# Attention weights kept in four tiles and stored from the diagonal; the keys' low parts formed for two heads at once

## The chip, the cores and the metric

The kernel runs on one core of a Trainium2 chip. The time is the device time of one execution in microseconds (us). A profiled execution shows the instructions of each engine: TensorE (PE, with its weight loads as a row of their own, PEld), VectorE (DVE), ScalarE (ACT), GpSimd (POOL), and SyncE (SP), whose queue issues most of the transfers between HBM and the on-chip memory. A time in a row counts from the first instruction, and L12 is line 12 of the kernel's file.

## The reference, cut to what matters

One layer of a transformer-like block over 1024 tokens of width 1024, all in float32: a layer norm, one input projection, two groups of heads that read it (4 gated-delta heads of 128 and 8 forgetting-attention heads of 64), an output projection, and a large MLP. The change touches the forgetting attention alone:

```python
def block(args):
    i, q_i, c_i = args
    s = jnp.einsum('bqhd,bkhd->bhqk', q_i, k).astype(jnp.float32) * scale
    s = s + c_i[..., :, None] - c_all[..., None, :]
    q_pos = i * Q_BLOCK + jnp.arange(Q_BLOCK)
    s = jnp.where(k_pos[None, :] <= q_pos[:, None], s, -jnp.inf)
    attn = jax.nn.softmax(s, axis=-1)
    return jnp.einsum('bhqk,bkhd->bqhd', attn.astype(v.dtype), v)
```

`c_all` is the running sum of the forget gates' logarithms. The scores are causal, in blocks of 128 queries.

## The kernel before, in words

TensorE multiplies in a rounded form of float32 (`F32R`). To come near full float32, an operand x is split into a high part (x rounded, by a copy on ScalarE) and a low part (x minus the high part, by `split_lo`, a subtraction on VectorE, L54), and a product becomes two or three matmuls: high with high, high with low, low with high.

The stages follow one another: layer norm and values, the projections in columns (`proj_ch`, L211, matmuls at L218), the gated-delta heads, the forgetting attention, the output projection (`tok_mm`, L955, matmuls at L958), and the MLP. The framework orders the instructions of each engine by priorities when the kernel is built, and each engine then runs its own list in that order; a load waits in SP's queue until its buffer is free, and what stands behind it waits too. The z projections (`z_proj`, L452, `gz` in the rows) have a late priority and fill TensorE while attention waits.

The attention (L701 to L902) is a loop over 64 steps (`steps`, L871): 8 heads times 8 query blocks r, in the order 0, 1, 4, 5, 2, 3, 6, 7. The parts of a step are spread over the loop's turns: `fox_a` of a step, `fox_b` of the step before, `fox_c` and `fox_d` of those before them.

- `fox_start` (L841) calls `fox_load` for a head, and for an even head `fox_values` for both heads of the pair. It is called four steps ahead of the head. `fox_load` (L710) brings in the head's queries and keys from `qk_spill`, each twice, to partitions 0 to 63 and 64 to 127 (L715, two tiles `raw` of tag `qk_raw`, of which there are two buffers). `qa` holds the high part of the queries above their low part (L719, L720), `ka` the high part of the keys twice (L721), `kl` the low part of the keys twice (L722, the `kl` rows of L54), and `cb` the gate sums, read to all partitions (L724). The tiles of even heads lie in the pool `fh[0]`, those of odd heads in `fh[1]`. The values of a pair (`vr`, L729) use tag `qk_raw` too, as do the raw loads of `gdn_mix` (L854).
- `fox_a` makes the scores of a query block, in one or two chunks of at most 512 keys: 128 rows of `qa` with `ka` (L753: high and low queries with high keys), 128 rows of `qa` with `kl` (L754: high and low queries with low keys), and where the chunk holds the diagonal, the causal mask as a bf16 matmul with the identity (L756). VectorE adds `cb` and takes the minimum (L758); ScalarE takes the exponential (L761).
- `fox_b` transposes the weights of the block, 128 by 128 (L783), into PSUM; ScalarE casts them into `pth`, the high part (L785), and VectorE subtracts into `ptl`, the low part (L786, rows of L54). Two query blocks, r = 2g and r = 2g + 1, make a group g and share the tiles `pth` and `ptl`, of shape [128, kmax, 2, 128]: key block, query block of the group, query. Groups 0 and 1 use tiles with kmax 4, groups 2 and 3 tiles with kmax 8, one buffer each. Key block nk - 1 (nk = 2g + 2) lies above the diagonal for the group's first query block, and GpSimd writes zeros there for each group (L776, L777).
- `fox_c` multiplies the values of each key block with the weights of both query blocks, for `pth` and `ptl` (L797), and `fox_d` transposes the result back (L808).

```python
pth = pool.tile([P, kmax, 2, P], F32R, tag=f"pt_hi{kmax}", name=f"pth{h}_{g}", bufs=1)
ptl = pool.tile([P, kmax, 2, P], F32R, tag=f"pt_lo{kmax}", name=f"ptl{h}_{g}", bufs=1)
nc.gpsimd.tensor_copy(out=pth[:, nk - 1, 0], in_=zero)
nc.gpsimd.tensor_copy(out=ptl[:, nk - 1, 0], in_=zero)
```

Elsewhere in the kernel nearly every matmul takes 128 rows. The one exception is a transpose of 50 rows ahead of the column stage (L339, `crow`, between the transposes of L167 and the value projection of L320).

Of the kernel before, what the change touches and what calls it, by code (L numbers as in the profile page):

```python
# [8 lines left out]
F32 = mybir.dt.float32  # L9
F32R = mybir.dt.float32r  # L10
# [5 lines left out]
P = 128  # L16
T = 1024
# [15 lines left out]
def _sl(i, n=P):  # L33
    return slice(i * n, (i + 1) * n)
# [3 lines left out]
def tile_block(ctx: ExitStack, tc: tile.TileContext, x, p, ln_in_g, ln_in_b, w_in, conv_w, a_log, dt_bias,  # L38
               gdn_norm_g, b_f, fox_norm_g, w_out, ln1_g, ln1_b, w_up, w_down, w_ple, w_ple_gate,
               b_ple_gate, ln2_g, ln2_b, out):  # L40
    nc = tc.nc
    PS = bass.MemoryType.PSUM
    x, p, out = x[0], p[0, 0], out[0]
# [9 lines left out]
    def split_lo(eng, lo, src, hi):  # L53
        eng.tensor_tensor(out=lo, in0=src, in1=hi.bitcast(F32), op=ALU.subtract)  # L54
# [27 lines left out]
    ident = cpool.tile([P, P], F32, name="ident")  # L82
# [3 lines left out]
    zero = cpool.tile([P, P], F32, name="zero")  # L86
# [17 lines left out]
    qk_spill = tc.dram_tile([2, 4, P, T], F32, name="qk_spill")  # L104
# [72 lines left out]
    def pj(name):  # L177

        return psd.tile([P, 512], F32, tag="pj", name=name)

    def sm(name):
        return psx.tile([P, 512], F32, tag="sm", name=name)
# [40 lines left out]
    with tc.tile_pool(name="start", bufs=2, reuse_waits="tile") as stp:  # L223
# [10 lines left out]
        pt = stp.tile([P, NT, DPLE], F32, name="p_raw", bufs=1)  # L234
# [35 lines left out]
        pth = stp.tile([P, 2, T], F32R, name="pT_hi", bufs=1)  # L270
        ptl = stp.tile([P, 2, T], F32R, name="pT_lo", bufs=1)
# [35 lines left out]
        for t in range(NT):  # L307
            if t + 3 < NT:
                load_x(t + 3)
            h = stp.tile([P, D], F32, tag="h", name=f"h{t}")  # L310
# [5 lines left out]
            for n in range(2):  # L316
                ps = pj(f"psv{t}")
                for k in range(NK):
                    for wi, (a, w) in enumerate(((act_hi, wv_hi), (act_hi, wv_lo), (act_lo, wv_hi))):
                        nc.tensor.matmul(ps[:, 0:264], a[t // 4][:, t % 4, k], w[:, k, _sl(n, 264)],  # L320
                                         start=(k == 0 and wi == 0), stop=(k == NK - 1 and wi == 2))
# [16 lines left out]
        ps = sm("ps_cols")  # L338
# [121 lines left out]
    for i in range(1, 3):  # L460
        nc.sync.dma_start(out=img[i].rearrange("(q r i) -> q r i", q=32, i=P),
                          in_=zero[0:32].unsqueeze(1).to_broadcast([32, GH * HST // (32 * P), P]))
# [239 lines left out]
    fp = fst.enter_context(tc.tile_pool(name="fox", bufs=2, reuse_waits="tile"))  # L702
    fh = [fst.enter_context(tc.tile_pool(name=f"foxh{j}", bufs=1, reuse_waits="tile")) for j in range(2)]
    fvp = fst.enter_context(tc.tile_pool(name="foxv", bufs=2, reuse_waits="tile"))
    frs = ExitStack()
    fr = frs.enter_context(tc.tile_pool(name="foxr", bufs=2, side="right", reuse_waits="tile"))
# [3 lines left out]
    def fox_load(h):  # L710
        pr, j = h // 2, h % 2
        raw = [fp.tile([P, T], F32, tag="qk_raw", name=f"qkr{h}_{w}", bufs=2) for w in range(2)]
        for w in range(2):
            for half in range(2):
                nc.sync.dma_start(out=raw[w][_sl(half, 64)], in_=qk_spill[w, pr, _sl(j, 64), :])  # L715
        qa = fh[j].tile([P, T], F32R, tag="qa", name=f"qa{h}")
        ka = fh[j].tile([P, T], F32R, tag="ka", name=f"ka{h}")
        kl = fh[j].tile([P, T], F32R, tag="kl", name=f"kl{h}")
        nc.scalar.copy(out=qa, in_=raw[0])  # L719
        split_lo(nc.vector, qa[64:128], raw[0][64:128], qa[64:128])  # L720
        nc.scalar.copy(out=ka, in_=raw[1])  # L721
        split_lo(nc.vector, kl, raw[1], ka)  # L722
        cb = fh[j].tile([P, T], F32, tag="cb", name=f"cb{h}")
        nc.sync.dma_start(out=cb, in_=row_spill[32 + h * 8:40 + h * 8, :].rearrange("c i -> (c i)").partition_broadcast(P))  # L724
        return qa, ka, kl, cb
# [11 lines left out]

    heads, pairs, tiles = {}, {}, {}

    def fox_a(h, r):  # L740

        j = h % 2
        qa, ka, kl, cb = heads[h]
        W = (r + 1) * P
        s = tiles[h, r] = fr.tile([P, T], F32, tag="s", name="s", bufs=2)
        m = fr.tile([P, 2], F32, tag="m", name="m", bufs=4)

        cut = min(W, 512) if W != 640 else 384
        for i, (n0, n1) in enumerate([(0, max(cut, 256)), (cut, W)][:1 + (W > 512)]):
            e = min(W, n1)  # L750
            diag = n0 <= r * P < n1
            ps = psf.tile([P, 512], F32, tag="sc", name="ps_sc")
            nc.tensor.matmul(ps[:, :n1 - n0], qa[:, _sl(r)], ka[:, n0:n1], start=True, stop=False)  # L753
            nc.tensor.matmul(ps[:, :n1 - n0], qa[:, _sl(r)], kl[:, n0:n1], start=False, stop=not diag)  # L754
            if diag:
                nc.tensor.matmul(ps[:, r * P - n0:(r + 1) * P - n0], identb, mask_f, start=False, stop=True)  # L756

            nc.vector.tensor_tensor_reduce(out=s[:, n0:e], in0=ps[:, :e - n0], in1=cb[:, n0:e], scale=1.0,  # L758
                                           scalar=3.0e38 if i == 0 else m[:, 0:1],
                                           op0=ALU.add, op1=ALU.min, accum_out=m[:, i:i + 1])  # L760
        nc.scalar.activation(out=s[:, :W], in_=s[:, :W], func=AF.Exp, bias=m[:, i:i + 1], scale=-1.0,  # L761
                             accum_out=pairs[h // 2][2][:, r, j:j + 1])

    def fox_b(h, r):

        g, rr = r // 2, r % 2
        nk = 2 * g + 2
        s = tiles.pop((h, r))
        if rr == 0:
            kmax = 4 if g < 2 else 8  # L770
            pool = fvp if kmax == 4 else fr
            pth = pool.tile([P, kmax, 2, P], F32R, tag=f"pt_hi{kmax}", name=f"pth{h}_{g}", bufs=1)
            ptl = pool.tile([P, kmax, 2, P], F32R, tag=f"pt_lo{kmax}", name=f"ptl{h}_{g}", bufs=1)
            tiles[h, "p"] = pth, ptl

            nc.gpsimd.tensor_copy(out=pth[:, nk - 1, 0], in_=zero)  # L776
            nc.gpsimd.tensor_copy(out=ptl[:, nk - 1, 0], in_=zero)  # L777
        pth, ptl = tiles[h, "p"]
        for k0 in range(0, r + 1, 4):
            kn = min(4, r + 1 - k0)  # L780
            pt = psf.tile([P, 512], F32, tag="pt", name="ps_pt").rearrange("q (c i) -> q c i", i=P)
            for i in range(kn):
                nc.tensor.transpose(pt[:, i], s[:, _sl(k0 + i)], ident)  # L783
            hi = pth[:, k0:k0 + kn, rr]
            nc.scalar.copy(out=hi, in_=pt[:, :kn])  # L785
            split_lo(nc.vector, ptl[:, k0:k0 + kn, rr], pt[:, :kn], hi)  # L786

    def fox_c(h, g):

        j = h % 2  # L790
        nk = 2 * g + 2
        va = pairs[h // 2][0]
        pth, ptl = tiles.pop((h, "c", g))
        po = psf.tile([P, 512], F32, tag="av", name="ps_av", bufs=1)
        for kb in range(nk):
            for i, pt in enumerate((pth, ptl)):
                nc.tensor.matmul(po[:, 0:256], va[j][:, kb].rearrange("q a d -> q (a d)"),  # L797
                                 pt[:, kb].rearrange("q a b -> q (a b)"),
                                 start=(kb == 0 and i == 0), stop=(kb == nk - 1 and i == 1))
        ot = tiles[h, "o", g] = fr.tile([P, 256], F32, tag="ot", name="ot")  # L800
        nc.scalar.copy(out=ot, in_=po[:, 0:256])
# [39 lines left out]
    def fox_start(h):  # L841
        heads[h] = fox_load(h)
        if h % 2 == 0:
            va = fox_values(h // 2)
            if h < 6:
                osb = fr.tile([P, 8, 2, DH], F32, tag="osb", name=f"osb{h}", bufs=3)
            else:
                osb = fvp.tile([P, 8, 2, DH], F32, tag="va", name=f"osb{h}", bufs=3)
            pairs[h // 2] = (va, osb,
                             fr.tile([P, 8, 2], F32, tag="ls", name=f"ls{h}"))  # L850
# [24 lines left out]
    for i in range(n + 12):  # L875
        if i < n:
            h, r = steps[i]
# [5 lines left out]
        if 1 <= i <= n:  # L883
            h, r = steps[i - 1]
# [3 lines left out]
        if 2 <= i < n + 2:  # L888
            h, r = steps[i - 2]
            if r % 2:  # L890
                fox_c(h, r // 2)
        if 3 <= i < n + 3:
            h, r = steps[i - 3]
# [97 lines left out]
    for t in range(NT):  # L991
        h1 = hpool.tile([P, D], F32, tag="h1", name=f"h1_{t}")
        nc.sync.dma_start(out=h1, in_=h_spill[_sl(t), :])
        j = t % 4
# [3 lines left out]
        for n in range(2):  # L998
            ps = early.get((t, n))
            if ps is None:  # L1000
                ps = pj("ps_mix")
# [312 lines left out]
    b = [bank("ps_db") for bank in (pj, pj, pj, sm)]  # L1314
    a = [sm("ps_da") for _ in range(4)]
# [110 lines left out]
    for js in ((0, 1), (2,), (3,)):  # L1426
        w = P * len(js)
        m = 512 // w
        for c0 in range(0, NP, m):
            r = x0[:, count["r"] % 4]  # L1430
# [4 lines left out]
            for i in range(m):  # L1435
                for wi, (x, y) in enumerate(((0, 0), (0, 1), (1, 0))):
                    for j in js:
                        nc.tensor.matmul(b[j], rs[x][:, i, _sl(j - js[0])], Q[c0 + i][y],  # L1438
                                         start=(c0 == 0 and i == 0 and wi == 0),
                                         stop=(c0 + i == NP - 1 and wi == 2))  # L1440
# [39 lines left out]
```

## Time and profile before

| | us |
|---|---|
| median of 3 runs (1426.23 to 1431.31) | 1428.26 |
| the profiled execution | 1429.82 |
| its span, first to last instruction | 1427.9 |
| TensorE busy, matmuls | 1381.4 |
| TensorE busy, weight loads | 1167.2 |
| VectorE busy | 1106.8 |
| ScalarE busy | 560.7 |
| GpSimd busy | 29.6 |

Busy time is the union of an engine's instructions. Matmuls are pipelined, and the end of each is modelled, so that a busy TensorE need not be at its peak; the distance from one start to the next says more. A row of the timeline gives start, duration, engine, line, operation, the tiles written and read, the shapes and, in brackets, the idle time of the engine before it and what ended that. "issue" means that nothing in the profile ended it. A share is given for the span; the page that goes with the profile gives the granted TensorE clock as full nearly throughout.

### The profile page before, as it was taken

The numbers are of one execution on the slowest core, as the hardware profiler recorded it, in microseconds if no ns is written. First come the engines' busy times: TensorE is split into PE (matmuls) and PEld (weight loads), VectorE is DVE, ScalarE is ACT, GpSimd is POOL, SyncE is SP. The second block draws the span as 40 slices with busy tenths as digits, with TensorE's granted clock in tenths as the row PEclk, the third lists the DMA queues.
The fourth block names the chain that finished last, engine by engine and source line by source line (L and its number), as shares of the span: only waits on it lengthen the run. The fifth ranks groups of instructions, "written<-read, shape, count | busy, mean of one in ns | idle before, by whom it ended". The sixth has DMA issues, their size and how long they took to land.

```text
span 1427.9 us, 20552 instructions
## 1 busy us (share of the span) xinstructions
PE 1381.4 (97%) x7342; PEld 1167.2 (82%) x7342; DVE 1106.8 (78%) x2326; ACT 560.7 (39%) x1024; POOL 29.6 (2%) x84
## 2 busy tenths in 40 slices
PE   7999989999999999899999999999999999999997
PEld 5988868988887888778889888888888888888885
DVE  6858799689478989968998677776667799747877
ACT  4324412241247777631134233333334444555421
POOL 1000000000000111100000000000000000000000
PEclk9999999999999999999999999999999999999999
DMA  9866425444553433433567744444445994334342
GB/s 301 247 178 208 133 76 130 150 159 122 136 167 112 132 99 115 141 121 129 198 232 220 222 158 162 142 150 148 137 159 197 315 325 147 96 96 126 114 137 81
DMA packets 195868, 229.09 MB, mean 160 GB/s; under 512 B 23877, under 2 KB 128566, under 8 KB 195766
## 3 DMA queue, kind: packets, MB, share of 16 engines
q1 hardware_dynamic: 186374, 221.48, 49.1%
q10 hardware_dynamic: 9008, 5.24, 1.4%
q8 instruction: 58, 0.95, 0.3%
q0 software_dynamic: 384, 1.06, 0.2%
q14 instruction: 44, 0.36, 0.1%
HBM read 152.14 MB, written 75.60 MB: 159 GB/s over the span
## 4 chain that ended last, share of the span: by engine, by line
PE 47%; DMA 4%; DVE 4%; issue 1%; ACT 0%; SPq 0%; DVEq 0%; ACTq 0%
PE ps_uP L1212 21%; PE ps_da L1332 9%; PE ps_db L1332 9%; PE ps_db L1438 3%; PE ps_mix L958 2%; DMA hb<-h_spill 1%; PE ps_gP L1079 1%; DVE h L51 1%; DMA r<-t_spill 1%; PE ps_tr L965 1%; DMA h_spill<-h 1%; DMA h<-h_spill 1%; DVE gv L51 0%; DVE st L140 0%; DMA wo_raw<-in_w_out_dram 0%
## 5 line engine op out<-in xcount | busy, mean ns | idle before, releaser
L1212 PE MATMUL ps_uP<-T,uS 128*128 128x512 f32 x576 | 133.9, 390 | 1.3 <-ACT ua L1217 1.3
L1212 PEld LDWEIGHTS ps_uP<-T,uS 128*128 128x128 f32 x576 | 108.1, 188 | 24.9 <-ACT ua L1217 1.7
L1302 ACT CAST rh<-rr 128x512 fp32r<-128x512 f32 x112 | 69.8, 623 | 139.6 <-PE ps_db L1332 51.9
L54 DVE TENSOR_TENSOR rl<-rr,rh 128x512 fp32r<-128x512 f32 x112 | 76.8, 687 | 60.3 <-ACT rh L1302 25.6
L1212 PE MATMUL ps_uP<-B,uA 128*128 128x512 f32 x384 | 92.2, 395 | 0.0
L1212 PEld LDWEIGHTS ps_uP<-B,uA 128*128 128x128 f32 x384 | 72.1, 188 | 17.3
L958 PE MATMUL ps_mix<-wo,act_hi 128*128 128x512 f32 x256 | 81.9, 396 | 0.3 <-ACT act_hi L838 0.3
L218 PE MATMUL g<-act_hi,in_hi 128*128 128x512 f32 x192 | 76.1, 396 | 5.0 <-DVE edge L431 5.0
L218 PE MATMUL g<-act_hi,in_lo 128*128 128x512 f32 x192 | 75.7, 396 | 1.1 <-DVE in_lo L54 1.1
L218 PE MATMUL g<-act_lo,in_hi 128*128 128x512 f32 x192 | 75.8, 395 | 0.0
L1302 ACT CAST rl<-B 128x512 fp32r<-128x512 f32 x96 | 59.6, 622 | 24.6 <-PE ps_db L1332 12.1
L54 DVE TENSOR_TENSOR uA<-uraw,uA 128x512 fp32r<-128x512 f32 x48 | 33.0, 689 | 46.2 <-ACT uA L1207 46.2
L1207 ACT CAST uS<-wS 128x512 fp32r<-128x512 f32 x64 | 39.5, 622 | 73.1 <-issue 48.2
L54 DVE TENSOR_TENSOR ql<-B,rl 128x512 fp32r<-128x512 f32 x96 | 65.5, 684 | 0.3
L54 DVE TENSOR_TENSOR ptl<-ps_pt,pth 128x512 fp32r<-128x512 f32 (+2 forms) x96 | 51.0, 551 | 8.7 <-ACT pth L785 8.0
L958 PEld LDWEIGHTS ps_mix<-wo,act_hi 128*128 128x128 f32 x256 | 47.4, 188 | 10.2 <-DVE wo L54 0.6
L51 DVE SCALAR_TENSOR_TENSOR cv<-g,hcw,cv 128x510 f32<-128x510 f32 (+2 forms) x72 | 53.2, 739 | 1.5 <-ACT cv L424 1.1
L785 ACT CAST pth<-ps_pt 128x512 fp32r<-128x512 f32 (+2 forms) x96 | 43.5, 480 | 22.1 <-PE ps_pt L783 21.0
L1332 PE MATMUL ps_da<-ql,rh 128*128 128x512 f32 x192 | 51.3, 389 | 0.0
L1332 PE MATMUL ps_db<-rl 128*128 128x512 f32 x192 | 51.3, 389 | 0.0
L1332 PE MATMUL ps_da<-rl 128*128 128x512 f32 x192 | 51.3, 389 | 0.0
L761 ACT ACTIVATE s<-s,m 128x128 f32<-128x128 f32 (+3 forms) x64 | 50.0, 781 | 3.4 <-DVE m L758 3.2
(369 smaller groups left out, 3628.6 us busy)
## 6 DMA issues: line engine op xcount, KB each, us to landing
uraw<-in_w_up_dram SPq DMA_DIRECT2D x32, 512.0 KB, 4.4
B<-in_w_down_dram SPq DMA_DIRECT2D x32, 512.0 KB, 5.3
rr<-rS SPq DMA_DIRECT2D x64, 256.0 KB, 2.8
in_raw<-in_w_in_dram SPq DMA_DIRECT2D x24, 512.0 KB, 4.1
rr<-rA SPq DMA_DIRECT2D x48, 256.0 KB, 2.8
h_spill<-h SPq DMA_DIRECT2D x16, 512.0 KB, 3.9
qkr<-qk_spill SPq DMA_DIRECT2D x32, 256.0 KB, 4.1
rA<-ub SPq DMA_DIRECT2D x32, 256.0 KB, 2.1
```

What stands on the lines that cost most here:

```text
L51: nc.vector.scalar_tensor_tensor(out=o, in0=a, scalar=s, in1=b, op0=op0, op1=op1)
L54: eng.tensor_tensor(out=lo, in0=src, in1=hi.bitcast(F32), op=ALU.subtract)
L218: mm = nc.tensor.matmul(ps, w[:, k, :], a[n][:, :, k], start=(k == 0 and wi == 0), stop=(k == NK - 1 and wi == 2))
L761: nc.scalar.activation(out=s[:, :W], in_=s[:, :W], func=AF.Exp, bias=m[:, i:i + 1], scale=-1.0, accum_out=pairs[h // 2][2][:, r, j:j + 1])
L785: nc.scalar.copy(out=hi, in_=pt[:, :kn])
L958: nc.tensor.matmul(ps, a[t // 4][:, t % 4, k], w, start=(k == 0 and wi == 0), stop=(k == NK - 1 and wi == 2))
L965: nc.tensor.transpose(ps[:, k], row[:, _sl(k)], ident)
L1207: nc.scalar.copy(out=hi, in_=a[s])
L1212: nc.tensor.matmul(ps[p], w[:, k], B[t][b][k], start=(chain is None and k == 0 and wi == 0), stop=(k == 3 and wi == 2), skip_group_check=c ...
L1302: nc.scalar.copy(out=hi, in_=src)
L1332: nc.tensor.matmul(ps[j], rs[x][:, _sl(j)], qs[y], start=(not chain and c == 0 and wi == 0), stop=(c == NP - 1 and wi == 2), skip_group_ch ...
L1438: nc.tensor.matmul(b[j], rs[x][:, i, _sl(j - js[0])], Q[c0 + i][y], start=(c0 == 0 and i == 0 and wi == 0), stop=(c0 + i == NP - 1 and wi ...
```

## The change

Two edits, both in the attention.

The weights' tiles are made once, ahead of the loop: a high and a low tile of kmax 4 and of kmax 8. They are kept for all heads. The key blocks are stored in reverse, from the diagonal back: key block kb of a group lies at place nk - 1 - kb. The place above the diagonal of the group's first query block is then always place 0, and GpSimd zeroes it once in each of the four tiles, 4 copies where there were 64. The transposes of a chunk are issued in reverse order, and `fox_c` reads place nk - 1 - kb.

The low part of the keys is formed once for a pair of heads. `qk_spill[1, pr]` holds the keys of both heads, 64 partitions each; for an even head they are loaded as they lie into a further raw tile of tag `qk_raw` (one load of 128 partitions), copied by ScalarE and subtracted in place by VectorE. The odd head takes over the tile, which lies in `fh[pr % 2]`. The second score matmul takes only the 64 partitions of its own head: high queries with low keys. To have the high queries on the same partitions, the low part of the queries goes to partitions 64 to 127 for an even head and 0 to 63 for an odd one. The product of the two low parts is no longer computed.

```diff
         qa = fh[j].tile([P, T], F32R, tag="qa", name=f"qa{h}")
         ka = fh[j].tile([P, T], F32R, tag="ka", name=f"ka{h}")
-        kl = fh[j].tile([P, T], F32R, tag="kl", name=f"kl{h}")
         nc.scalar.copy(out=qa, in_=raw[0])
-        split_lo(nc.vector, qa[64:128], raw[0][64:128], qa[64:128])
+
+        lo = _sl(1 - j, 64)
+        split_lo(nc.vector, qa[lo], raw[0][lo], qa[lo])
         nc.scalar.copy(out=ka, in_=raw[1])
-        split_lo(nc.vector, kl, raw[1], ka)
+        if j == 0:
+
+            kr = fp.tile([P, T], F32, tag="qk_raw", name=f"qkr{h}_l", bufs=2)
+            nc.sync.dma_start(out=kr, in_=qk_spill[1, pr])
+            kl = fh[pr % 2].tile([P, T], F32R, tag="kl", name=f"kl{h}")
+            nc.scalar.copy(out=kl, in_=kr)
+            split_lo(nc.vector, kl, kr, kl)
+        else:
+            kl = heads[h - 1][2]
...
+    weights = []
+    for kmax, pool in ((4, fvp), (8, fr)):
+        weights.append([pool.tile([P, kmax, 2, P], F32R, tag=f"pt_{part}{kmax}", name=f"pt{part[0]}{kmax}", bufs=1)
+                        for part in ("hi", "lo")])
+        for w in weights[-1]:
+            nc.gpsimd.tensor_copy(out=w[:, 0, 0], in_=zero)
...
-            nc.tensor.matmul(ps[:, :n1 - n0], qa[:, _sl(r)], kl[:, n0:n1], start=False, stop=not diag)
+            nc.tensor.matmul(ps[:, :n1 - n0], qa[_sl(j, 64), _sl(r)], kl[_sl(j, 64), n0:n1], start=False, stop=not diag)
...
         if rr == 0:
-            kmax = 4 if g < 2 else 8
-            pool = fvp if kmax == 4 else fr
-            pth = pool.tile([P, kmax, 2, P], F32R, tag=f"pt_hi{kmax}", name=f"pth{h}_{g}", bufs=1)
-            ptl = pool.tile([P, kmax, 2, P], F32R, tag=f"pt_lo{kmax}", name=f"ptl{h}_{g}", bufs=1)
-            tiles[h, "p"] = pth, ptl
-
-            nc.gpsimd.tensor_copy(out=pth[:, nk - 1, 0], in_=zero)
-            nc.gpsimd.tensor_copy(out=ptl[:, nk - 1, 0], in_=zero)
+            tiles[h, "p"] = weights[g // 2]
         pth, ptl = tiles[h, "p"]
         for k0 in range(0, r + 1, 4):
             kn = min(4, r + 1 - k0)
             pt = psf.tile([P, 512], F32, tag="pt", name="ps_pt").rearrange("q (c i) -> q c i", i=P)
+            m0 = nk - k0 - kn
             for i in range(kn):
-                nc.tensor.transpose(pt[:, i], s[:, _sl(k0 + i)], ident)
-            hi = pth[:, k0:k0 + kn, rr]
+                nc.tensor.transpose(pt[:, i], s[:, _sl(k0 + kn - 1 - i)], ident)
+            hi = pth[:, m0:m0 + kn, rr]
             nc.scalar.copy(out=hi, in_=pt[:, :kn])
-            split_lo(nc.vector, ptl[:, k0:k0 + kn, rr], pt[:, :kn], hi)
+            split_lo(nc.vector, ptl[:, m0:m0 + kn, rr], pt[:, :kn], hi)
...
-                                 pt[:, kb].rearrange("q a b -> q (a b)"),
+                                 pt[:, nk - 1 - kb].rearrange("q a b -> q (a b)"),
```

## Rows read from the trace of the kernel before

**Rows 1.** Windows of the attention: stretch, length, each engine's busy us (instructions), clock, DMA.

```profile
418.00:570.00 152.00, 150.22 (x965) 125.32 (x964) 131.35 (x359) 110.73 (x254) 18.31 (x54) 1.00 0.39 119
570.00:600.00 30.00, 24.88 (x157) 20.68 (x155) 27.93 (x68) 21.15 (x43) 3.49 (x6) 0.94 0.50 158
600.00:625.00 25.00, 24.02 (x151) 19.97 (x150) 19.07 (x38) 15.92 (x32) 1.06 (x4) 1.00 0.31 106
```

**Rows 2.** Timeline of TensorE around 475 us: start us, duration us, engine, line.

```profile
474.05 0.28 PE L753 MATMUL ps_sc<-ka,qa 128*128 128x256 f32 x1
474.06 0.19 PEld L754 LDWEIGHTS ps_sc<-kl,qa 128*128 128x128 f32 x1
...
474.17 0.28 PE L754 MATMUL ps_sc<-kl,qa 128*128 128x256 f32 x1
...
475.19 0.39 PE L754 MATMUL ps_sc<-kl,qa 128*128 128x512 f32 x1
...
475.41 0.39 PE L218 MATMUL gz<-act_lo,in_hi 128*128 128x512 f32 x1
```

**Rows 3.** The chain that ended last, around 625 us: start us, us, what.

```profile
622.30 0.39 PE ps_av L797
...
625.04 11.83 PE ps_mix L958 x51
```

**Rows 4.** Groups by line, 418 to 625 us: count, busy us, mean ns, idle before, releasers.

```profile
L776 POOL CAST pth<-zero 128x128 fp32r<-128x128 f32 x32 | 14.8, 464 | 340.2 <-PE ps_o L651 170.0 <-PE ps_av L797 128.3 <-DVE ptl L54 18.3
...
L777 POOL CAST ptl<-zero 128x128 fp32r<-128x128 f32 x32 | 9.8, 307 | 0.0
...
L721 ACT CAST ka<-qkr 128x1024 fp32r<-128x1024 f32 x6 | 6.4, 1065 | 0.0
```

**Rows 5.** Waits, 418 to 625 us: waiter, releaser, us in total, times, longest.

```profile
ACT pth L785 <- PE ps_pt L783: 21.0, 29, 1.5
...
DVE ptl L54 <- POOL pth L776: 0.3, 1, 0.3
```

**Rows 6.** The tile kl: its writers, ns shortest, median and longest, first and last start.

```profile
L54 DVE TENSOR_TENSOR kl<-qkr,ka x8: 1215/1220/1226, 401.3 to 575.8; 128x1024 fp32r<-128x1024 f32 x8
```

**Rows 7.** DMA issues: count, size of each, median us to landing.

```profile
vr<-v_spill SPq DMA_DIRECT2D x4, 512.0 KB, 5.0
```

**Rows 8.** Timeline of VectorE: the kl splits of head 2 and of head 7.

```profile
448.00 1.22 DVE L54 TENSOR_TENSOR kl<-qkr,ka 128x1024 fp32r<-128x1024 f32 x1
...
575.81 1.22 DVE L54 TENSOR_TENSOR kl<-qkr,ka 128x1024 fp32r<-128x1024 f32 x1
```

**Rows 9.** Line 753 from 418 to 466.35 us: loads and matmuls, first and last start.

```profile
L753 PEld LDWEIGHTS ps_sc<-ka,qa x25: 186/190/202, 418.2 to 466.3; 128*128 128x128 f32 x25
L753 PE MATMUL ps_sc<-ka,qa x24: 277/404/498, 418.4 to 463.8; 128*128 128x512 f32 x10, 128*128 128x256 f32 x8, 128*128 128x384 f32 x6
```

**Rows 10.** Line 754, 418 to 570 us, then 570 to 625 us.

```profile
L754 PE MATMUL ps_sc<-kl,qa x80: 274/338/400, 418.5 to 567.9; 128*128 128x512 f32 x32, 128*128 128x256 f32 x28, 128*128 128x384 f32 x20
...
L754 PE MATMUL ps_sc<-kl,qa x16: 277/376/398, 576.4 to 612.3; 128*128 128x512 f32 x8, 128*128 128x384 f32 x4, 128*128 128x256 f32 x4
```

**Rows 11.** Timeline of TensorE around the 50-row transpose (x8: eight in one row).

```profile
89.26 0.90 PEld L167 LDWEIGHTS ps_tr<-ident,h 128*128 128x128 f32 x8
89.37 1.04 PE L167 MATMUL ps_tr<-ident,h 128*128 128x128 f32 x8
...
90.33 0.14 PEld L339 LDWEIGHTS ps_cols<-ident,crow 50*128 50x128 f32 x1 [0.17 <-issue]
90.33 0.26 PE L339 MATMUL ps_cols<-ident,crow 50*128 50x50 f32 x1
...
90.64 0.19 PEld L320 LDWEIGHTS psv<-wv_hi,act_hi 128*128 128x128 f32 x1 [0.17 <-ACT act_hi L169]
```

**Rows 12.** Waits of the weight loads over the whole span, two of those by issue.

```profile
PEld L756 <- issue: 6.0, 27, 0.3
...
PEld ps_cols L339 <- issue: 0.2, 1, 0.2
```

## The prediction

> **What bounds the kernel now.** I read the windows first, to place the stage that the change touches. Attention runs from 418 to 625 us of the span. Up to 570 us TensorE is busy for 150.22 of 152 us, which leaves 1.78 us idle. From there to 600 us it is idle for 5.12 us while VectorE is busy for 27.93 of 30, and to 625 us for another 0.98: 6.10 us in all [rows 1]. A busy row alone doesn't show that TensorE is full, since matmuls overlap, so the timeline comes next. There the starts follow one another without a hole: a 256-column score matmul 0.12 us after the one before it, a 512-column one 0.22 us before the next, and the projection matmuls (L218) fill in wherever attention has nothing ready. Each weight load starts with the matmul in front of it and lies under it [rows 2]. So two stretches differ. Before 570 us the time is TensorE's: what is added to its queue lengthens the stage one for one, and what is taken off VectorE there is worth nothing. After 570 us the filler has run out, VectorE is the fuller engine, and TensorE has room. The chain of waits says whether that matters for the end: it runs over attention's last value matmuls and goes straight on into the output projection [rows 3]. A shift of the stage's end is a shift of the kernel's end, and I pass it on whole.
>
> **Part one, the kept weight tiles.** The change removes 64 zeroing copies on POOL (14.8 and 9.8 us of busy time) and issues 4, of some 0.3 us each [rows 4]. POOL does little else there, and all that anybody waited for it is 0.3 us of VectorE, once [rows 5]. Worth: 0 to 0.3 us gained; I take 0.3. Storing the blocks from the diagonal changes no count, shape or engine: the transposes (L783), casts (L785) and subtractions (L54) stay as many and as large, and so do the value matmuls (L797). The one new freedom is that a write into a kept tile waits for the matmuls that read that tile, where before it waited for a new buffer of a pool; ScalarE's casts waited for their own transposes, 21.0 us in 29 waits, and no row has them waiting for a value matmul [rows 5]. I cost this at nothing. Its cover is the alternation of the small and the large tile pair from group to group; without it a cast would wait for one group's value matmuls.
>
> **Part two, low key parts for two heads, on the other engines.** VectorE now makes 8 splits of 128x1024 for kl, at 1.22 us each; it will make 4. ScalarE gains 4 copies of the same size as L721's, about 1.06 us each. SP gains 4 loads of 512 KB, which as vr take 5.0 us to land [rows 4, 6, 7]. VectorE's 4.9 us count only after 570 us, and there lies one kl split, head 7's, at 575.81 [rows 8]: 1.2 us gained at most, 0 if the stretch waits for something else; I take 1.2. ScalarE's 4.2 us count nothing while it stays the lightest of the three. The new load stands in SP's queue behind the key loads, with a wait for the raw buffer that the query split gives back; queued behind it are the head's cb, the pair's vr, the next head's raw loads, the z_spill stores and the loads of w_out. The cover is the lead of a head: head 2's kl split, the third, starts at 448.00 and ends at 449.2 us, and its first score comes after the 24 of heads 0 and 1, with a weight load at 466.3 [rows 8, 9]. Load, copy and split (5.0, 1.06 and 1.22) come to 7.3 us against 17.1, so I cost it at nothing here. If that cover were gone, the price would be up to 7.3 us at each of three later pairs.
>
> **Part two, on TensorE.** The second score matmul (L754) drops from 128 rows to 64, at partitions 0 or 64 by the head. Columns and count stay: 96 of them, 80 before 570 us and 16 after [rows 10]. Nothing gets shorter that the rows could show, since the starts are spaced by columns [rows 2]. What is new is that TensorE goes from 128 rows to 64 and back 96 times, in the middle of its fullest stretch.
>
> The trace has one instruction to price this, the 50-row transpose of L339 [rows 11]. Eight 128-row transposes ran before it, their weight loads back to back from 89.26 for 0.90 us, so to 90.16. The 50-row weight load began at 90.33: 0.17 us idle that nothing released, where loads normally start under the matmul in front. By matmul starts the loss is smaller: the eight, 0.11 us apart from 89.37, would have been followed at 90.25, and L339 started at 90.33, so 0.08 us. Idle time without a releaser is rare on this queue. Apart from the bf16 identity's loads, with 27 such waits, L339 is one of nine groups with one or two each in the whole span [rows 12]; that its only occurrence has one is hardly chance. So 0.08 to 0.17 us for the way in. The way out is open: the next load came at 90.64, after 0.17 us idle, but ScalarE's act_hi had just come, so it costs between 0 and 0.17 us. Per matmul that makes 0.08 to 0.34 us. Both readings of the one switch are equally near, so I take the middle, 0.21 us. A rule of the Trainium skill goes further than the row (TensorEngine Tiling (Array Packing), Key Properties): changing the tiling mode, not only the tile, drains TensorE, and by it the way out would cost like the way in, 0.34 us in all. By that rule the sum below would be +28.4 us; no row here shows the way out alone.
>
> **The sum.** Before 570 us: 80 x 0.21 = +16.8. After it, 16 x 0.21 = 3.4, of which I let half vanish in the 6.10 us of idle time: +1.7. VectorE's split: -1.2. POOL: -0.3. Together +17.0 us. The profiled execution took 1429.8 us (span 1427.9 and 1.9 around it), 1.6 above the median of the runs shown, so +17.0 gives 1446.8 for it and **1445.3 us** against the median. The bounds in the same way: at 0.08 us, 6.4 + 0.6 - 1.5 = +5.5, 1433.8; at 0.34 us, 27.2 + 2.7 - 1.5 = +28.4, 1456.7.
>
> **Rivals.** *No stall* (faster, or the same). Place: the weight load of L754. If a 64-row load slips under a running 128-row matmul as a 128-row one does, TensorE's part is zero and -1.5 us is left, 1426.8; if the lighter VectorE also closes all of the 6.10 us of idle time, 1422.2. It decides below 1.5 / 80 = 0.02 us per switched matmul; under that the kernel is not slower. For it: 64 and 128 rows stream the same columns, and one event is thin evidence. Against it: that event. A table of the Trainium skill is on this side (TensorE: Matmul & The Clock Gate, Why this matters for your kernels): a matmul over 32 rows alone takes the same time as one over 128; the trace has no such matmul in a stream.
>
> *The load chain.* The extra raw load makes a later head's keys or w_out late: three pairs at up to 7.3 us each, so up to +21.9, 1450.2 without any stall. For it: both rings are two deep and SP waits in order. Against it: the 17.1 us of lead.
>
> *The change does less than it says.* If the 64-row matmul is run as a 128-row one and the split that is saved was covered, nothing is left: 1428.3. For it speaks only that every saved piece lies off TensorE.
>
> **How the numbers follow.** A measurement of this kernel can tell 0.3%, 4.3 us, from no change. A stall as I priced it: 0.70, of which 0.67 is slower by more than that and 0.03, at the lowest price, lies within it. No stall: 0.24, split 0.13 faster (the idle time closes too) and 0.11 the same. Load chain: 0.04, slower. Nothing left: 0.02, the same. That makes 0.13 faster, 0.16 the same, 0.71 slower. The likeliest case has its own range of 1433 to 1457. The whole range reaches down to 1425, into the cases without a stall, and up to 1459; about 0.12 is left below and 0.06 above.
>
> **What would show it.** Right: L754's weight load no longer starts with L753's matmul but 0.1 us or more after that one's stream has ended, with idle time of the load queue before it put to issue, 96 times; the load behind it lags in the same way; and the stretch of 80 score matmuls grows by 6 to 27 us with VectorE less full in it. The kl group halves to 4 splits and POOL's casts fall to 4. Wrong: L754 keeps its 0.12 and 0.22 us of distance to its neighbours; then the stage ends where it did, or a little earlier, and the sum was wrong at the switch. If TensorE instead waits for kl or qa at the heads' first scores, the load chain was the mechanism. If it waits for a cast that waits for value matmuls, the kept tiles cost what I put at nothing.

## The result, and the profile after

The changed kernel takes 1454.87 us (median of 4 runs, 1453.39 to 1456.23) against 1428.08 us for the kernel before (the three runs of the table above and a fourth): a ratio of 1.0179 with an interval of [1.0162, 1.0195]. The medians differ by 26.8 us; the interval of the ratio is 23.1 to 27.8 us. The profiled execution took 1456.23 us, with a span of 1454.5.

In the new numbering the score matmuls are L770 (128 rows) and L771 (the low key parts, now 64 rows), the mask L773, the transposes L794, the casts L796, the value matmuls L808, the zeroing copies L755. The first line is the page's busy time: VectorE and POOL have less to do (1106.8 and 29.6 us before), ScalarE more (560.7 before), and TensorE's busy time has grown from 1381.4.

```profile
PE 1412.0 (97%) x7342; PEld 1173.0 (81%) x7342; DVE 1103.5 (76%) x2322; ACT 566.2 (39%) x1028; POOL 8.7 (1%) x24
```

Next, the windows of the attention (stretch, length, then busy time and instructions of TensorE, its weight loads, VectorE, ScalarE and POOL, then clock, DMA share, GB/s):

```profile
418.00:570.00 152.00, 151.92 (x844) 112.58 (x842) 113.08 (x313) 102.19 (x227) 1.90 (x4) 1.00 0.42 123
570.00:600.00 30.00, 29.15 (x168) 21.88 (x166) 24.61 (x71) 20.74 (x46) 0.00 (x0) 1.00 0.42 124
600.00:625.00 25.00, 22.50 (x128) 16.91 (x127) 19.59 (x44) 16.29 (x33) 0.00 (x0) 0.86 0.31 96
625.00:660.00 35.00, 33.47 (x182) 26.84 (x181) 23.73 (x55) 15.07 (x30) 0.00 (x0) 1.00 0.36 121
```

Compare the first line with [rows 1]: TensorE is still busy all the time, but in the same 152 us it gets through 844 matmuls where it did 965. Every matmul is there; they have become slower to follow one another. VectorE and ScalarE fall back with it (313 instructions for 359, 227 for 254): they wait for TensorE. The stage reaches into the fourth window, as the value matmuls of L808 say (the writers of the tile ps_av: count, ns shortest, median and longest, first and last start):

```profile
L808 PE MATMUL ps_av<-ptl,va x160: 276/281/562, 436.3 to 649.1; 128*128 128x256 f32 x160
```

and in the kernel before:

```profile
L797 PE MATMUL ps_av<-ptl,va x160: 274/283/418, 433.2 to 623.8; 128*128 128x256 f32 x160
```

The last one starts at 649.1 us; before, the last one of L797 started at 623.8. So 25.3 of the 26.6 us by which the span grew were lost by the end of the attention. From the first score matmul's start to this last start the attention took 205.5 us before and takes 230.3 now, 24.8 us more.

The third window's clock of 0.86 can carry little of it. It comes from one stretch at the lower of the two clock levels, behind a hole in TensorE's work; here are the windows around it, and around the same thing in the kernel before:

```profile
605.00:610.00 5.00, 2.84 (x19) 1.94 (x17) 3.59 (x5) 5.00 (x10) 0.00 (x0) 0.92 0.00 0
610.00:615.00 5.00, 4.69 (x18) 3.63 (x19) 3.74 (x9) 2.02 (x6) 0.00 (x0) 0.50 0.75 250
```

```profile
575.00:580.00 5.00, 3.07 (x19) 2.31 (x18) 5.00 (x14) 3.49 (x8) 0.00 (x0) 0.96 0.65 220
580.00:585.00 5.00, 4.48 (x26) 3.83 (x25) 3.60 (x10) 2.26 (x6) 0.53 (x2) 0.70 0.47 154
```

By such windows of 5 us, from 570 to 655 us, the clock was at 1.2 GHz instead of 2.4 for 6.9 us in the kernel after and for 3.4 before. At half speed the 3.5 us between them are worth some 1.8 us at most. The kernel of experiment 2 has 3.5 us of it and the same loss.

The timeline of TensorE shows how the time is lost. This is the kernel after, start us, duration us, engine, line:

```profile
475.47 0.19 PEld L770 LDWEIGHTS ps_sc<-ka,qa 128*128 128x128 f32 x1
475.49 0.42 PE L770 MATMUL ps_sc<-ka,qa 128*128 128x384 f32 x1
475.84 0.18 PEld L771 LDWEIGHTS ps_sc<-kl,qa 64*128 64x128 f32 x1 [0.19 <-issue]
475.85 0.44 PE L771 MATMUL ps_sc<-kl,qa 64*128 64x384 f32 x1
476.21 0.19 PEld L218 LDWEIGHTS gz<-act_hi,in_hi 128*128 128x128 f32 x1 [0.19 <-issue]
476.22 0.50 PE L218 MATMUL gz<-act_hi,in_hi 128*128 128x512 f32 x1
476.32 0.19 PEld L770 LDWEIGHTS ps_sc<-ka,qa 128*128 128x128 f32 x1
```

The load of L770 starts at 475.47 and its matmul 0.02 us later. The 64-row load does not start under that matmul, as L754's did in [rows 2]: it starts 0.35 us after it, with 0.19 us of idle time that no engine released, and its own matmul follows 0.01 us later. Then the same happens on the way out: the projection's 128-row load (L218) waits from 475.85 to 476.21, again with 0.19 us by issue. The load behind it starts 0.10 us after L218's matmul: among 128-row loads, the next one slips under the matmul in front again. The waits, from 418 to 652 us, count it (waiter, releaser, us in total, times, longest):

```profile
PEld ps_sc L771 <- issue: 17.4, 69, 0.4
PEld L773 <- issue: 6.6, 31, 0.2
PEld gz L218 <- issue: 2.8, 13, 0.2
```

L771 waits so 69 times of its 96. The rows leave out short waits: in the trace, idle time stands before all 96 loads, 20.9 us in all. Before, L754 had no such row; over the whole span L756, the mask, had 27 [rows 12].

What the change meant to save, it saved. These are the writers of kl in the kernel after, then POOL's groups by line:

```profile
L728 ACT CAST kl<-qkr_l x4: 1042/1052/1055, 405.5 to 550.9; 128x1024 fp32r<-128x1024 f32 x4
L54 DVE TENSOR_TENSOR kl<-qkr_l,kl x4: 1218/1220/1226, 407.2 to 553.0; 128x1024 fp32r<-128x1024 f32 x4
```

```profile
L755 POOL CAST pth<-zero 128x128 fp32r<-128x128 f32 x2 | 1.4, 712 | 180.5 <-PE ps_o L651 169.9 <-DMA o_spill<-vb 10.6
L755 POOL CAST ptl<-zero 128x128 fp32r<-128x128 f32 x2 | 0.6, 296 | 0.0
```

Four splits where there were eight [rows 6], four zeroing copies where there were 64 [rows 4].

### The profile page after: what moved, and what is told of

Same layout as the page of the kernel before. It is cut to its first block, busy times and chain, and to the rows that moved or that the text cites. A ratio compares the mean times of both kernels' runs of the same rounds, so it can differ in the third digit from the quotient of the medians.

```text
span 1454.5 us, 20407 instructions
## 1 busy us (share of the span) xinstructions
PE 1412.0 (97%) x7342; PEld 1173.0 (81%) x7342; DVE 1103.5 (76%) x2322; ACT 566.2 (39%) x1028; POOL 8.7 (1%) x24
## 5 line engine op out<-in xcount | busy, mean ns | idle before, releaser
L218 PE MATMUL g<-act_hi,in_hi 128*128 128x512 f32 x192 | 76.4, 398 | 5.5 <-DVE edge L431 5.5
L218 PE MATMUL g<-act_hi,in_lo 128*128 128x512 f32 x192 | 76.1, 398 | 0.5 <-DVE in_lo L54 0.5
L218 PE MATMUL g<-act_lo,in_hi 128*128 128x512 f32 x192 | 76.0, 396 | 0.0
L796 ACT CAST pth<-ps_pt 128x512 fp32r<-128x512 f32 (+2 forms) x96 | 43.9, 479 | 36.3 <-PE ps_pt L794 35.6
L775 DVE CUSTOM_DVE_ANT_0 s<-ps_sc,cb 128x384 f32<-128x384 f32 (+2 forms) x64 | 36.3, 569 | 25.3 <-PE ps_pt L794 20.9
L1343 PE MATMUL ps_db<-rl,rh 128*128 128x512 f32 x192 | 51.3, 389 | 0.0
L1343 PE MATMUL ps_db<-ql,rh 128*128 128x512 f32 x192 | 51.3, 389 | 0.0
```

The costliest lines, as they stand in the source:

```text
L218: mm = nc.tensor.matmul(ps, w[:, k, :], a[n][:, :, k], start=(k == 0 and wi == 0), stop=(k == NK - 1 and wi == 2))
L1343: nc.tensor.matmul(ps[j], rs[x][:, _sl(j)], qs[y], start=(not chain and c == 0 and wi == 0), stop=(c == NP - 1 and wi == 2), skip_group_ch ...
```

## The experiments

The theory from here on: the 64-row matmul makes TensorE change its mode twice per visit, and that is all of the loss. Mode is the theory's word for what sets a 64-row matmul apart from a 128-row one. Against it stood the rest of the change (the load, the copy, the kept tiles), and, within the theory, the questions of what counts as another mode, what a visit costs, and where part of the cost goes. A visit is one 64-row matmul, or several in a row, between 128-row ones.

**1. All of the change but the 64 rows.** On the kernel after; the low parts of the other head then meet the other half of qa, so the scores hold a product too many.

```
-            nc.tensor.matmul(ps[:, :n1 - n0], qa[_sl(j, 64), _sl(r)], kl[_sl(j, 64), n0:n1], ...)
+            nc.tensor.matmul(ps[:, :n1 - n0], qa[:, _sl(r)], kl[:, n0:n1], ...)
```

> The changed kernel with its second score matmul over all 128 rows again; everything else of the change stays. The 128 rows add one product that the reference doesn't have, low queries of the head with low keys of the pair's other head, which is as small as rounding. Switch theory (each of the 96 visits to 64 rows costs TensorE 0.3 to 0.4 us, because weight loads can't slip under a running matmul on the way in and out): the whole loss goes, 1423 to 1428 us, a ratio of 0.996 to 1.000 to the kernel before, and the score matmuls are spaced 0.12 and 0.23 us as before. Rest theory (the extra raw load, the kept tiles or the new order of the queues cost the time): the time stays above 1445 us.

Measured: 1429.58 us, ratio 1.001 [0.9999, 1.002]. The loss is gone, so load, copy, shared splits and kept tiles cost nothing that can be seen (2.9 us at most, by the interval). But they gain nothing either, where the expectation had up to 5 us. The windows of this kernel, as above:

```profile
570.00:600.00 30.00, 24.70 (x150) 19.95 (x149) 25.61 (x64) 20.48 (x41) 0.00 (x0) 0.94 0.53 153
600.00:625.00 25.00, 23.96 (x153) 20.19 (x152) 19.14 (x40) 15.95 (x32) 0.00 (x0) 1.00 0.35 111
```

VectorE is busy 2.3 us less than in the second of [rows 1], and TensorE is idle as before (5.3 us for 5.1). The chain that ended last says what the end of the attention hangs on instead (start us, us, what):

```profile
616.67 5.22 DMA wo_raw<-in_w_out_dram
...
621.91 0.36 ACT wo L961
...
622.86 0.59 ACT pth L796
...
623.50 0.39 PE ps_av L808
```

A load of w_out lands at 621.9, its copy (L961, 1.05 us) runs ahead of the last cast pth in ScalarE's queue, and the last value matmuls wait for that cast. The kernel before has the same chain up to the row of [rows 3] at 622.30. A lighter VectorE does not move it here.

**2. Only the 64 rows.** On the kernel before; it leaves out the products of the rows from 64 on, which hold part of the low corrections.

```
-            nc.tensor.matmul(ps[:, :n1 - n0], qa[:, _sl(r)], kl[:, n0:n1], ...)
+            nc.tensor.matmul(ps[:, :n1 - n0], qa[0:64, _sl(r)], kl[0:64, n0:n1], ...)
```

> The kernel before with one edit: the second score matmul takes partitions 0 to 63 alone (high queries with low keys; the product of the low parts is left out). Keys, tiles and zeroing as before. Switch theory: the loss is all there, 1452 to 1458 us, ratio 1.017 to 1.021, slightly more than the change since VectorE's splits aren't saved. Rest theory: 1426 to 1433 us.

Measured: 1454.46 us, ratio 1.0191 [1.0174, 1.0207]. One edit to one line carries the whole loss. Its waits repeat the pattern of the kernel after:

```profile
PEld ps_sc L754 <- issue: 17.8, 74, 0.4
PEld L756 <- issue: 6.2, 29, 0.2
```

This kernel keeps the order of the kernel before, so its starts can be set against that one's, place by place. From the start of the 128-row score matmul to the start of the second matmul behind the 64-row one, medians, before and here: 256 columns with a mask behind, 0.30 and 0.59 us (30 places); 384 columns with a mask, 0.39 and 0.68 (13); 512 columns with a mask, 0.51 and 0.88 (15); with a projection matmul behind, 0.39 us more (16 places). Taken place by place, the differences with a mask are 0.28, 0.29 and 0.30 us in the median for the three widths. With the 16 before a projection that makes 0.31 us for a visit. A second count agrees: against the kernel of experiment 4, which has the same order and loses nothing, TensorE's matmuls up to the second one behind each visit come 24.3 us late in all for the 80 visits ahead of 570 us, 0.30 each. The sums below take 0.30.

Of the 0.39 us before a projection, 0.09 are lost on the way in, 0.19 on the way out, and 0.10 because the first 128-row load has not run under anything, so that the load behind it is late too. With a mask behind, only the first two are lost.

**3. Only the kept tiles.** On the kernel before: the four weight tiles made and zeroed once, the blocks stored from the diagonal.

```
+    weights = []
+    for kmax, pool in ((4, fvp), (8, fr)):
...
+            nc.gpsimd.tensor_copy(out=w[:, 0, 0], in_=zero)
...
+            tiles[h, "p"] = weights[g // 2]
```

> The kernel before with the kept tiles alone: four tiles, zeroed once, blocks from the diagonal; keys as before, 128 rows. Switch theory: 1426 to 1429 us, ratio 0.998 to 1.001, since POOL's zeroing was waited for by 0.3 us. Rest theory: above 1433 us if the kept tiles make casts wait for value matmuls.

Measured: 1426.67 us, ratio 1.0 [0.999, 1.0011]. Sixty zeroing copies fewer and no new wait: nothing, in either direction.

**4. Ninety-six rows.** On the kernel before; leaves out the products of the last 32 rows.

```
+            nc.tensor.matmul(ps[:, :n1 - n0], qa[0:96, _sl(r)], kl[0:96, n0:n1], ...)
```

> The kernel before with one edit: the second score matmul takes partitions 0 to 95 (half of the product of the low parts is left out). If the cost comes with any matmul of fewer than 128 rows (row theory), the time is like that with 64 rows, 1452 to 1458 us. If it comes with a change of the array's row mode, and 96 rows still fill the 128-row mode (switch theory), the time is that of the kernel before, 1426 to 1430 us, and the weight loads start under the matmul in front as before.

Measured: 1428.58 us, ratio 1.0005 [0.9995, 1.0015]. The timeline of TensorE:

```profile
474.11 0.28 PE L753 MATMUL ps_sc<-ka,qa 128*128 128x256 f32 x1
474.12 0.19 PEld L754 LDWEIGHTS ps_sc<-kl,qa 96*128 96x128 f32 x1
474.23 0.28 PE L754 MATMUL ps_sc<-kl,qa 96*128 96x256 f32 x1
```

The 96-row load starts 0.01 us after the matmul in front, as a 128-row one does. That fewer rows than the matmul in front have a price as such is refuted: 96 rows run with 128 for nothing, 64 do not. A rule of the Trainium skill fits both (TensorEngine Tiling (Array Packing), Key Properties): a change of tiling mode, not merely of tile, drains TensorE. The trace agrees for 64 rows, at some 0.30 us for in and out. That 96 rows run like 128 is what this experiment shows by its time and its loads; no row names a mode.

**5. Both 64-row matmuls of a block in a row.** On the kernel after: per block of rows first all ka matmuls into two banks, then all kl matmuls, to pay for one visit in place of two.

```
+        for ps, (n0, n1) in zip(banks, chunks):
+            nc.tensor.matmul(... ka[:, n0:n1], start=True, stop=False)
+        for ps, (n0, n1) in zip(banks, chunks):
+            nc.tensor.matmul(... kl[_sl(j, 64), n0:n1], start=False, ...)
```

> The changed kernel, where a query block with two chunks of keys issues its two 128-row score matmuls first and then its two 64-row ones, so that TensorE goes to 64 rows and back 64 times instead of 96; the 64-row matmuls stay 96. Switch theory (the price is per visit): a third of the loss goes, 1444 to 1448 us, ratio 1.011 to 1.015, and in the trace the second 64-row matmul of a pair follows the first at the spacing of its columns, 0.23 us for 512, with its weight load under the first. Row theory (the price is per 64-row matmul): the time stays at 1453 to 1457 us.

Measured: 1455.01 us, ratio 1.0182 [1.0155, 1.0209]: no gain. The trace says why: only 9 of the 32 pairs stand next to each other on TensorE, which leaves 87 visits for 96. The order of the program's text is not the order of the queue. Its runs also show a lower granted clock, 0.987 to 0.990 where those of the changed kernel show 0.992 to 0.994. The experiment did not test what it was for.

**6. The same, with the order held.**

```
-            nc.tensor.matmul(ps[:, :n1 - n0], qa[:, _sl(r)], ka[:, n0:n1], start=True, stop=False)
+            last = nc.tensor.matmul(ps[:, :n1 - n0], qa[:, _sl(r)], ka[:, n0:n1], start=True, stop=False)
+        with tc.issue_after(last.ins):
```

> The grouped kernel again, with the 64-row matmuls of a block queued behind its last 128-row score matmul on TensorE, so that the pairs stand together (nearly all 32 of them, some 65 to 70 visits for 96 matmuls; without the queueing only 9 pairs did). Switch theory: some 30 visits of 0.3 to 0.4 us less than the change, so 9 to 11 us less on TensorE; 1444 to 1447 us, ratio 1.011 to 1.014, or somewhat more where the bound scores wait for the second bank. Row theory: 1453 to 1457 us.

Measured: 1447.05 us, ratio 1.0126 [1.0112, 1.0139], with 65 visits and still 96 matmuls of 64 rows. Against the kernel after, 31 visits fewer gave back some 8 us (1.0179 less 1.0126, of 1428), or 0.25 us each. That is the lower of two readings. Three of the four runs show a granted clock of 0.989 or 0.990 and took 1446.2 to 1448.0 us; the profiled one, at 0.994, took 1443.95. In the profiled executions the attention takes 219.5 us for 230.3 in the kernel after, which is 0.35 us for each visit saved. By either reading the price is one of visits and not of 64-row matmuls. The timeline shows a pair (x2 are two in a row), and the waits stand behind it:

```profile
477.87 0.29 PEld L772 LDWEIGHTS ps_sc<-kl,qa 64*128 64x128 f32 x2 [0.25 <-issue]
477.87 0.61 PE L772 MATMUL ps_sc<-kl,qa 64*128 64x512 f32 x2
478.41 0.10 PEld L776 LDWEIGHTS <-identb 128*128 128x128 bf16 x1 [0.25 <-issue]
```

```profile
PEld L776 <- issue: 10.7, 42, 0.4
PEld ps_sc L772 <- issue: 10.4, 41, 0.4
```

Two loads lie within 0.29 us: the second slips under the first 64-row matmul. In and out cost 0.25 us of idle load time each, and the waits of the 64-row loads fall from 69 to 41.

**7 and 8. Which visits show in the time.** On the kernel before, 64 rows for the last two heads alone (24 visits, among them the 16 of which the prediction let half vanish), and for the first six (72 visits). Both leave out the products of the rows from 64 on in those heads.

```
+            n = 64 if h >= 6 else P
+            nc.tensor.matmul(ps[:, :n1 - n0], qa[0:n, _sl(r)], kl[0:n, n0:n1], ...)
```

(for the second, `h < 6`)

> The kernel before, 64 rows in the second score matmul of heads 6 and 7 alone (24 visits; the product of the low parts is left out there). At the 0.34 us that the changed kernel's trace gives on average per visit, TensorE has 8.1 us more to do. If the idle time after 570 us takes up half or more of that (the prediction's step for the tail), the kernel is 2 to 4 us slower, 1430 to 1432 us; if nothing is absorbed, 8 us, 1436 us; in proportion to the count alone it would be 6.7 us.

> The kernel before, 64 rows in the second score matmul of heads 0 to 5 alone (72 visits; the product of the low parts is left out there). At 0.34 us per visit 24.5 us more on TensorE, in the stretch where it has no idle time: 1450 to 1453 us if nothing is absorbed, 1448 us (20.1 us) in proportion to the count alone.

Measured: 1433.91 us, ratio 1.0033 [1.0017, 1.0049], for the last two heads; 1446.21 us, 1.0119 [1.0098, 1.014], for the first six. Neither is what was expected: the first lies between its two cases, the second below both. At 0.30 us a visit they cost TensorE 7.2 and 21.6 us; 4.7 and 17.0 show.

TensorE's starts say where the rest goes, since these kernels too keep the order of experiment 4's. From the first score matmul to the place that lies at 570 us in the kernel before, the kernel with 64 rows for the first six heads falls 19.4 us behind in its 72 visits, and the one with 64 rows in all heads 21.5 us in 80. That is 0.27 us each, so a tenth of the price is made good between the visits. The last 16, behind that place, cost 2.9 us with 64 rows in all heads and 1.6 us with 64 rows in the last two, in place of 4.8. So a good part of the last 16 is absorbed, and a little of the visits far ahead of the idle stretch as well.

The idle time of the windows accounts for little of the second part. Ahead of 570 us TensorE was idle for 0.8 us in the kernel of experiment 4 and is for 0.1 us in the kernel with 64 rows for the first six heads; there the hole of [rows 1] only comes later:

```profile
570.00:600.00 30.00, 28.03 (x176) 22.83 (x175) 26.84 (x72) 20.69 (x45) 2.13 (x8) 0.98 0.44 130
600.00:625.00 25.00, 21.82 (x145) 18.38 (x145) 22.95 (x50) 17.81 (x37) 3.99 (x8) 0.95 0.30 91
```

The waits of the weight loads may. These are two rows of the kernel before, 418 to 627 us, then the same two of the kernel with only the 64 rows, 418 to 652 us:

```profile
PEld ps_oq L808 <- ACT ot L801: 6.2, 19, 1.5
...
PEld ps_sc L753 <- DVE m L758: 2.4, 4, 1.6
```

```profile
PEld ps_oq L808 <- ACT ot L801: 2.5, 8, 0.8
...
PEld ps_sc L753 <- DVE m L758: 0.7, 1, 0.7
```

A TensorE that is slowed down finds ScalarE's and VectorE's results ready more often. Summed over all rows with a releaser, from 418 us to the end of the attention, these waits were 17.1 us before, and 18.0, 15.2 and 15.9 in the kernels of experiments 1, 3 and 4, which lose nothing. They are 9.2 us with 64 rows in all heads, 11.5 with the first six, 14.2 with the last two, the last of these hardly outside that spread. The direction fits, the sizes do not match one by one: by the starts 4.5 us are missing with all heads, 2.2 with the first six and 4.0 with the last two. That these very waits pay is a reading of the traces, and no run takes one of them away.

**9 and 10. What the end of the attention hangs on.** The second half of w_out is loaded without the head start that the scheduler gave it, first on the kernel of experiment 1, then on the kernel before with nothing else changed.

```
-        wo = [load_half(w_out, n, wot, f"wo{n}") for n in range(2)]
+        wo = [load_half(w_out, 0, wot, "wo0")]
+    with tc.high_priority(offset=0):
+        wo.append(load_half(w_out, 1, wot, "wo1"))
```

> The first experiment (shared low keys, kept tiles, 128 rows) with one more edit: the second half of the output projection's weights is loaded without a raised priority, so that ScalarE's last two copies of it stand behind the last cast of attention weights in its queue. Tail theory (VectorE's saved splits brought nothing because the end of attention hangs on the last load of w_out, whose copy stands before that cast): attention's last value matmuls come 1 to 3 us earlier, and the kernel takes 1423 to 1427 us, ratio 0.997 to 0.999. Rival (the output projection then waits for the late weights itself): 1428 to 1435 us.

> The kernel before with the late loads of w_out alone (keys, tiles and zeroing as before). If the small gain of the ninth experiment came from the load order, this one has it too: ratio 0.997 to 0.9995. If it came from the shared low keys together with that order (VectorE's saved splits count once the load no longer sets the end), this one is at 0.9995 to 1.001.

Measured: 1428.03 us, ratio 0.9986 [0.9975, 0.9996], with VectorE's saved splits; 1427.3 us, 0.9988 [0.9976, 0.9999], without them. The two are the same to within some 2 us, so the little gain (some 2 us, barely clear of the noise and below what the prediction called a difference) goes with the loads, and the four saved splits are worth nothing that shows, with the loads out of the way too. In the second kernel no load of w_out stands in the chain that ended last, and the value matmuls end 2.4 us earlier than in the kernel before, at 621.4 for 623.8:

```profile
L797 PE MATMUL ps_av<-ptl,va x160: 277/282/562, 435.2 to 621.4; 128*128 128x256 f32 x160
```

That end alone proves little: in the kernel of experiment 3, whose ratio is 1.0 and whose chain still holds the load, they end at 621.7. By the ratio these two are the fastest kernels of the study, by little, and neither has the 64-row matmul.

## Why the prediction was right, and where it was off

**The mechanism and the sign were right.** The 64-row load no longer starts with the matmul in front of it, the idle time before it is put to issue, and the load behind it lags in the same way; the kl splits halve, POOL's casts fall to 4, and VectorE is less full, as the prediction said its profile would show. 1454.87 lies in the range, 9.6 us above the number.

**The price of a visit was mis-sized: 0.21 us was taken, 0.30 is measured.** The step that failed is the one from the single 50-row transpose to "the middle" of 0.08 and 0.34. The upper end was nearer, for two reasons. The prediction left the way out open, at 0 to 0.17 us, because ScalarE's act_hi had come just then [rows 11]; the way out waits 0.19 to 0.25 us in the runs. And the smaller reading, 0.08 us by matmul starts, took in only the way in: that is what the way in measures here too (0.09 us), but the exit, and before a projection the exposed load behind it, come on top. In the prediction's sum, 80 visits and half of 16, the difference of 0.09 us is 7.9 us. The range held because its upper bound took the way out as dear as the way in; the number in its middle was a choice between two readings.

The prediction gave the rule of the Trainium skill (TensorEngine Tiling (Array Packing), Key Properties), that a mode change drains TensorE, a sum of its own, +28.4 us; of its three sums the measured +26.8 is nearest to that.

**The term for idle time was about right behind 570 us, and missing ahead of it.** It let half of the 16 visits behind 570 us vanish because TensorE is idle there, and put the 80 before it down one for one. By the starts 40% (64 rows in all heads) to two thirds (the last two) of the 16 visits' cost vanish. Of the 80, 0.27 us each is left of 0.30, together 2.9 us less. So "before 570 us the time is TensorE's" holds for nine tenths of what was added there. The row with 150.22 of 152 us busy [rows 1] can hide waits of the load queue that lie under a matmul's modelled end; that it is these which shrink is not shown.

**VectorE's split was worth 0, not 1.2 us.** The prediction named the condition (0 if the stretch waits for something else), and the something else is the load of w_out and its copy (experiment 1). With that out of the way the splits still gained nothing that shows, though 1.2 us would be hard to see there (9 and 10).

**POOL, the kept tiles and the load chain, at 0.3 us and at nothing, were right** to within what can be measured (experiments 1 and 3).

With the terms as experiment 2's kernel shows them by its starts, the sum is 21.5 us for the 80 visits, 2.9 for the 16 and nothing for the rest: +24.3. The attention of the changed kernel, in another order and another run, is 24.8 us longer. The medians differ by 26.8 us, and the interval from 23.1 to 27.8 holds both. What the further 2 us are is open; the profiled executions differ by as much where the kernels are alike (the first score matmul starts at 418.1 to 422.5 us).

**The rivals.** No stall falls with the timeline. The table of the Trainium skill that stood for it (TensorE: Matmul & The Clock Gate, Why this matters for your kernels: a matmul over 32 rows alone takes as long as one over 128) is about a matmul by itself; no run here has a 32-row one, and among 128-row matmuls a 64-row one costs its visit. The load chain falls with experiment 1, which has the additional loads and loses nothing. That the change does less than it says falls with the rows: 64-row loads, four splits and a longer time.

## What to carry to other kernels

Before rows are cut from a matmul in the middle of a full TensorE stream, look at what its neighbours use: 64 rows among 128-row matmuls cost some 0.30 us at each visit here and save nothing, while 96 rows cost nothing. If the smaller matmul is needed, put several in a row and hold that order in the queue, since the visit is what is paid. And when a single event in a trace shows a new kind of stall, count the way out and the load behind it as well as the way in before taking a middle value.

## What was not expected of the hardware

That the rows have a step rather than a slope: 96 rows follow 128 at the old spacing (0.12 us at 256 columns), 64 rows do not. And that within a run of 64-row matmuls loads slip under matmuls as usual: the second load of a pair lies within the 0.29 us of the two.
